# Low halves of weights made by ScalarE and an accumulating DMA instead of VectorE

## The chip, the cores and the metric

The kernel runs on one core of one Trainium2 chip. The metric is the device time of one execution in microseconds (us); a time is the median of several runs. Engines are named as in the profile: PE is TensorE's matrix product, PEld its weight load, DVE VectorE, ACT ScalarE, POOL GpSimd, and SP the engine that issues most of the DMAs.

## The reference

A small diffusion backbone of two layers over 512 latent tokens (and 256 context tokens in layer 0), all in float32. Each layer is FFN, mixer, FFN; the mixer is attention in layer 0 and a gated short convolution in layer 1. Each part has an RMS norm with shift, scale and gate (adaLN) that come from a conditioning vector through a large matrix.

```python
def modulate(x, g, shift, scale):
    return rmsnorm(x, g) * (1 + scale) + shift

def swiglu(x, w_gate, w_up, w_down):
    return (jax.nn.silu(x @ w_gate) * (x @ w_up)) @ w_down

def macaron_ffn(xs, g, shift, scale, gate, w_gate, w_up, w_down):
    return xs + 0.5 * gate * swiglu(modulate(xs, g, shift, scale), w_gate, w_up, w_down)
...
    for i in range(DEPTH):                       # DEPTH = 2
        m = jnp.split((jax.nn.silu(c) @ mod_w[i] + mod_b[i])[:, None, :], N_MOD, axis=-1)
        ...
        x_lat = macaron_ffn(x_lat, norm_g[i, 0], m[0], m[1], m[2], ...)
        ...                                      # attention or convolution, with m[3], m[4], m[5]
        x_lat = macaron_ffn(x_lat, norm_g[i, 2], m[6], m[7], m[8], ...)
    return rmsnorm(x_lat, final_g)
```

The model width is 1024 (8 chunks of 128), the FFN's inner width 2816 (22 chunks of 128).

## The kernel before

Activations lie feature-major: a tile holds 128 features by up to 512 tokens. Every matrix product has float32 precision and is made of three products in the faster float32r type: weight and input are each split into a high part (rounded to float32r) and a low part (the remainder), and PE adds up high x high, high x low and low x high (`mm3`). So each weight tile of 128 x 1024 costs 24 products of 128x128 with 512 tokens.

A weight comes in by `load_w`: SP issues the load into a tile `raw`; ACT writes the high half `wh` (L114); an engine, nearly always DVE, writes the low half `wl` as raw minus high (L115). Each of `raw`, `wh` and `wl` has three buffers. A `raw` buffer is free again when both halves are written, a `wh` or `wl` buffer when PE has done its last product with it.

The FFNs are numbered: 0 and 1 in layer 0, 2 and 3 in layer 1. FFN 1, 2 and 3 work alike, on the latent tokens alone. The 22 inner chunks are cut into blocks of 4, 4, 4, 6 and 4. For each chunk of a block `gate_up` loads a gate and an up weight (two tiles of 1024 columns), lets PE make both products into one PSUM tile `S` (of which there are two), and ACT and DVE make SiLU(gate) x up and split it again (`out`, tiles `P` and `h`). After each block but the last `down` loads the block's part of the down matrix, in 4 units of 1024 columns for a block of 4, in 8 units of 768 columns for the block of 6, and DVE adds the result to `x` (L470). The first three weights of an FFN (`head`), the up weight of chunk 1 (`after_head`) and the last block's down weights (`tail`) go through other functions.

Beside the FFN bodies runs the adaLN work: each `gate_up` of FFN 1 and 2 calls `background(2)`, two steps of `mod_step`. A step loads two tiles of 256 KB of the adaLN matrix (`aux`, four buffers, L197, issued by SP) and DVE sums their products with the conditioning vector (L210). FFN 3 has none.

The code is written in program order; a scheduler places each instruction on its engine's queue by its own estimate of when it can run, so the order of a queue isn't that of the code. Each engine runs its queue strictly in order, and SP issues its DMAs in order too: a load that waits for its buffer holds back all that stand behind it.

Of the kernel before, what the change touches and what calls it, by code (L numbers as in the profile page):

```python
# [18 lines left out]
KD = D // P            # chunks of the model width  # L19
N = 512                # latent tokens  # L20
NC = 256               # context tokens
# [7 lines left out]
BLOCKS = [(0, 4), (4, 4), (8, 4), (12, 6), (18, 4)]   # (first f chunk, chunks)  # L29
BLOCKS0 = [(0, 6), (6, 6), (12, 6), (18, 4)]                  # layer 0, first FFN  # L30
# [11 lines left out]
def build(tc, A, out):  # L42
    """A: name -> DRAM AP (host layouts, see kernel()); out: [128, 8, 512] feature-major."""
# [4 lines left out]
    with ExitStack() as es:  # L48
# [9 lines left out]
        def uid(s):  # L58
# [4 lines left out]
        BUFS = {"xn": 16, "h": 12, "P": 4,                                                 # 3 KB per partition  # L63
                "x": 12, "sc": 2, "pj": 6, "pv": 4, "P1": 4, "aux": 4,                     # 2 KB
                "nh": 7}                                                                   # 1 KB
# [7 lines left out]
        def tmp(n):  # L73
            """temporary of a norm"""
            if n > 256:
                return dt_("pj")
            return dp.tile([P, 256], F32, tag="nh", bufs=BUFS["nh"], name=uid("nh"))

# [16 lines left out]
        wl_eng = [nc.vector]  # L95

        def load_wx(src, tiles, lo):
            """in halves of 512 columns; tiles: two for each part"""
# [10 lines left out]
        def load_w(src, n=1024, eng=None):  # L109
            raw = wp.tile([P, 1024], F32, tag="raw", bufs=3, name=uid("raw"))  # L110
            nc.sync.dma_start(raw[:, :n], src)
            hi = wp.tile([P, 1024], F32R, tag="wh", bufs=3, name=uid("wh"))
            lo = wp.tile([P, 1024], F32R, tag="wl", bufs=3, name=uid("wl"))
            nc.scalar.activation(hi[:, :n], raw[:, :n], AF.Copy)  # L114
            (eng or wl_eng[0]).tensor_tensor(lo[:, :n], raw[:, :n], hi[:, :n], op=ALU.subtract)  # L115
            return hi, lo

        def split(hi, lo, src, scale=None):
            """hi + lo == src * scale exactly (scale a power of two)"""
# [9 lines left out]
        def after_mm(i):  # L129
            """not scheduled before the last matrix product emitted so far"""  # L130
# [4 lines left out]
        def mm3(outs, w, x, segs, first, last):  # L135
            """outs[i] += w^T x[:, segs[i]] with the three products that float32 needs"""
# [17 lines left out]
        wx = [dt_("x", dtype=F32R) for _ in range(4)]           # for weights of the start  # L154
# [4 lines left out]
        def load_c(nm):  # L159
            """silu of the vector on every partition"""  # L160
# [31 lines left out]
        def mod_step(l, m, ch, dve, pool=(), paced=True, early=False):  # L192
            """the streams in dve are summed on the vector engine, those in pool on GpSimd and ScalarE"""
# [38 lines left out]
        def mod_scale(l, m, i, s="c", out=None, ks=slice(0, KD)):  # L232
            """norm_g * (1 + scale)"""
# [6 lines left out]
        def rsqrt(ps, n, width):  # L240
            """(ps / width + eps) ** -0.5, with one Newton step after the table"""
# [10 lines left out]
        class Norm:  # L252
            """sum of squares gathered chunk by chunk (two partial sums), then 1/rms on every partition"""
# [5 lines left out]
            def add(self, xk, pre=False):  # L259
                """pre: have the table of rsqrt loaded by the time the sum is there"""  # L260
                n, i = self.n, min(self.k // 4, 1)
                if self.k >= self.parts:            # summed on the tensor engine
                    i = len(self.ss)
                    self.ss.append(None)
# [17 lines left out]
        def modulate_chunk(k, xk, y, s, b, hi, lo):  # L282
# [3 lines left out]
            if n <= 256 and k % 3 == 2:             # a part of them on ScalarE and GpSimd  # L286
# [12 lines left out]
        class Entry:  # L299
            """the input of a sub-layer: modulated norm of x, one token segment at a time"""  # L300
# [26 lines left out]
        class Head:  # L327
            """first products of a sub-layer, k outermost and one token segment at a time,
            so that they run while the rest of the input is still being made"""

            def __init__(self, units):
                # units: [(weight source, {segment: PSUM})], the PSUM allocated when used
                self.w = [load_w(u[0]) for u in units]
                self.units = units

            def run(self, e, si, ks=range(KD), inner=False):
                """inner: k innermost, so that the weights are freed one after the other"""
# [9 lines left out]
        def transition(e, down, head):  # L347
            """down(si): last products of the sub-layer before, segment si (calls e.norms[si].add);
            head(): makes the Head; statistics and products of neighbouring segments overlap"""
# [26 lines left out]
        def last_proj(e, srcs, nk, hl, evict):  # L376
            """output projection with nk chunks of input: the last three weight units are kept and used
            one token segment at a time"""
# [27 lines left out]
        class FFN:  # L406
# [6 lines left out]
            def head(self):  # L413
                """gate and up of chunk 0, gate of chunk 1"""
# [18 lines left out]
            def gate_up(self, e, f, segs, halves=False):  # L433
                fi = self.fi
                ws = (load_w(A["wg"][fi, f]), load_w(A["wu"][fi, f]))
# [21 lines left out]
            def after_head(self, e):  # L457
                """finish chunk 1 (its up product); returns with chunks 0 and 1 done for the latents"""
# [18 lines left out]
            def down(self, bi):  # L477
# [3 lines left out]
                for d0 in range(0, KD, dpu):  # L481
                    w = load_w(*self.down_src(bi, d0))
# [7 lines left out]
            def body(self, e, first=2):  # L490
                """everything up to the last block's gate and up"""
# [10 lines left out]
            def tail(self, e2):  # L502
                """down products of the last block, one segment at a time"""
# [4 lines left out]
                held = {}                       # the three units loaded last  # L508
# [36 lines left out]
        # ================= layer 0: FFN 0 =================  # L545
        # the latents' part of the first chunks starts as soon as its modulation is there
# [83 lines left out]
        # ================= layer 0: attention =================  # L630
# [13 lines left out]
        # the residual waits in DRAM  # L644
# [4 lines left out]
        # differential lambda on every partition  # L649
# [22 lines left out]
        def proj_fm(src, outs):  # L672
            """outs: (segment, what takes the result) one after the other"""
# [9 lines left out]
        def proj_v(src, res, stack):  # L683
            """256 columns of a value projection, token-major, 3 tiles of 128 tokens per buffer: hi and lo in
            buffers of their own, or (stack) for each head of width 64 side by side, the second head lo first"""
# [30 lines left out]
        # Two heads (or maps) of width 64 share a chunk. For each, the moving operand stacks the  # L716
        # hi and lo parts of k over the 128 rows of the array and the stationary one holds hi of q
        # twice, so that one product gives qh kh + qh kl; ql kh is a second one on 64 rows.
# [3 lines left out]
        def q_parts(q, src, dst, scale):  # L722
            """src: 128 rows; dst: column view to write"""
# [32 lines left out]
        def scores(key, parts):  # L756
            """for (out, m, qs, ks) in parts: out = q k^T of head or map m, query columns qs, key columns given by
            the view ks; the products on 64 rows come together (outs in different banks)"""
# [64 lines left out]
        class Diff:  # L823
            """two query tiles of one differential head"""
# [77 lines left out]
        # neighbourhood heads: token order t' = column * 8 + row; query tiles are  # L902
        # A = columns 0-7 and 56-63, 1 = 8-23, 2 = 24-39, 3 = 40-55, so that tiles 1..3
        # see exactly the key columns 16(j-1) .. 16(j-1)+31 and A sees 0-15 and 48-63.
        def na_bias(h):
            """[128, 512]: columns 0-255 for tiles 1..3, 256-511 for tile A"""
            b = dt_("aux")
            nc.gpsimd.memset(b, -1e30)
            wn = A["rpb"][h]                        # [8 rq, 31 * 8]
# [7 lines left out]
        class Na:  # L917
            """one neighbourhood head: rows 64 i .. of pair pr"""
# [42 lines left out]
            def values(self):  # L961
# [14 lines left out]
                def transposes(step):  # L976
                    pt = acc("pv")
                    dsts = []
                    if step < 2:                        # context keys, all queries
                        src = [Ps[t][:, 256 + step * P:256 + (step + 1) * P] for t in range(4)]  # L980
                        dsts = [(4 + step, 0, N, o)]
                    else:                               # band keys, the two tiles that see the chunk
# [31 lines left out]
                # rows R hold the product with hi of v, the other half that with lo  # L1014
# [10 lines left out]
        def alternate(a, b):  # L1025
            """scores and values in turn, spread evenly: (unit, generator) each"""
# [24 lines left out]
        pos = [0.0, 0.0]                        # time on the tensor engine: attention, projections  # L1051
# [51 lines left out]
        # ================= layer 0: FFN 1 =================  # L1103
# [5 lines left out]
        # ================= layer 1: FFN 0 =================  # L1109
# [7 lines left out]
        # ================= layer 1: short convolution =================  # L1117
# [43 lines left out]
        # ================= layer 1: FFN 1, final norm =================  # L1161
# [100 lines left out]
```

## Time and profile before

| | |
|---|---|
| median of 3 runs | 2298.47 us (2294.9 to 2307.2) |
| span of the profiled execution | 2304.0 us (no other time of that execution is on the page) |
| PE busy | 2224.3 us, 97% of the span |
| DVE, ACT, POOL busy | 60%, 38%, 12% |
| DMA: bytes, mean rate | 279.07 MB, 121 GB/s |
| bodies of FFN 1, 2, 3 in the span, about | 1030 to 1370, 1390 to 1740, 1940 to 2280 us |

A row of a group names line, engine, operation and tiles, then count, busy time and mean of one in ns, then the idle time of the engine just before such instructions and what ended most of it. A row of waits names who waited for what: total us, times, longest. A row of the timeline gives start and duration in us, and in brackets the idle time before it with its releaser.

### The profile page before, as it was taken

What the parts mean: (1) busy time and instruction counts of PE and PEld (TensorE: products, weight loads), DVE (VectorE), ACT (ScalarE), POOL (GpSimd) and SP (SyncE); (2) the same over time, 40 slices, a digit from 0 to 9 for tenths busy, and PEclk for the clock granted to TensorE, in tenths of its full rate; (3) what the DMA queues carried; (4) which work ended last, traced back from release to release, by engine and by line L of the source; (5) the groups of instructions that cost most, each with busy time, mean ns of one, the idle gap of its engine ahead of it and who ended that gap; (6) DMA issues with size and microseconds to landing.
All of it is one profiled execution on the core that took longest, in us unless ns stands there. A gap on an engine that the chain in (4) does not pass through costs nothing.

```text
span 2304.0 us, 30465 instructions
## 1 busy us (share of the span) xinstructions
PE 2224.3 (97%) x11728; PEld 1889.3 (82%) x11728; DVE 1372.8 (60%) x2388; ACT 869.8 (38%) x1489; POOL 284.1 (12%) x196
## 2 busy tenths in 40 slices
PE   5899999999989999999999999999999999999998
PEld 3688888888878788788888888888889889888887
DVE  8893763534788876775555467555437446434335
ACT  4651421212456766652222244222225224222224
POOL 4550520000232311120000010000001001000001
PEclk9999999999999999999999999999999999999999
DMA  7672443434520111315555454444332322333232
GB/s 243 220 230 90 140 133 105 149 103 128 160 69 29 48 39 53 101 48 165 172 169 165 143 163 156 156 159 152 109 107 95 100 93 92 93 100 96 87 109 74
DMA packets 109993, 279.07 MB, mean 121 GB/s; under 512 B 14100, under 2 KB 18452, under 8 KB 109848
## 3 DMA queue, kind: packets, MB, share of 16 engines
q1 hardware_dynamic: 109848, 277.13, 38.5%
q8 instruction: 91, 1.49, 0.3%
q14 instruction: 54, 0.44, 0.1%
HBM read 272.88 MB, written 4.19 MB: 120 GB/s over the span
## 4 chain that ended last, share of the span: by engine, by line
PE 84%; DVE 10%; ACT 3%; issue 2%; POOL 1%; DMA 1%; SPq 0%; DVEq 0%; ACTq 0%; POOLq 0%
PE S L140 39%; PE acc L140 38%; PE acc L694 3%; DVE junk L210 1%; DVE wl L115 1%; PE S L763 1%; DVE xn L292 1%; PE acc L973 1%; DVE sm L215 1%; PE S L761 1%; PE acc L997 1%; DVE nh L285 1%; ACT wh L114 0%; POOL P L205 0%; PE acc L888 0%
## 5 line engine op out<-in xcount | busy, mean ns | idle before, releaser
L140 PE MATMUL S<-xn,wh 128*128 128x512 f32 (+1 forms) x3008 | 924.8, 380 | 20.8 <-ACT xn L291 12.5
L114 ACT ACTIVATE wh<-raw 128x1024 fp32r<-128x1024 f32 (+1 forms) x354 | 364.5, 1031 | 1072.2 <-PE acc L140 516.5
L140 PEld LDWEIGHTS S<-xn,wh 128*128 128x128 f32 x3008 | 555.9, 189 | 135.6 <-ACT xn L291 15.5
L115 DVE TENSOR_TENSOR wl<-raw,wh 128x1024 fp32r<-128x1024 f32 (+1 forms) x331 | 398.8, 1206 | 430.9 <-ACT wh L114 428.1
L140 PE MATMUL S<-xn,wl 128*128 128x512 f32 (+1 forms) x1504 | 569.0, 378 | 6.3 <-DVE wl L115 6.3
L140 PE MATMUL acc<-h,wh 128*128 128x512 f32 (+1 forms) x2148 | 534.6, 347 | 2.9 <-DVE x L470 2.8
L140 PE MATMUL acc<-xn,wh 128*128 128x256 f32 (+1 forms) x1664 | 451.1, 332 | 3.7 <-ACT xn L291 1.6
L140 PEld LDWEIGHTS acc<-h,wh 128*128 128x128 f32 x2148 | 364.2, 190 | 59.4 <-ACT h L121 3.1
L140 PE MATMUL acc<-h,wl 128*128 128x512 f32 (+1 forms) x1074 | 345.0, 344 | 1.4 <-DVE wl L115 1.4
L140 PEld LDWEIGHTS S<-xn,wl 128*128 128x128 f32 x1504 | 285.0, 190 | 61.5 <-DVE wl L115 8.3
L140 PEld LDWEIGHTS acc<-xn,wh 128*128 128x128 f32 x1664 | 297.1, 193 | 32.1 <-issue 2.7
L140 PE MATMUL acc<-xn,wl 128*128 128x256 f32 (+1 forms) x832 | 273.1, 329 | 3.2 <-DVE wl L115 3.2
L470 DVE SCALAR_TENSOR_TENSOR x<-acc,sm,x 128x512 f32<-128x512 f32 (+1 forms) x216 | 132.2, 629 | 220.1 <-PE acc L140 219.8
L140 PEld LDWEIGHTS acc<-h,wl 128*128 128x128 f32 x1074 | 192.4, 189 | 26.4 <-DVE wl L115 1.8
L270 POOL TENSOR_TENSOR nh<-nh,nh 128x256 f32<-128x256 f32 x42 | 45.4, 1085 | 1233.2 <-ACT nh L266 898.8
L210 DVE SCALAR_TENSOR_TENSOR junk<-aux,sc 128x512 bf16<-128x512 f32 x256 | 192.6, 752 | 1.6
L140 PEld LDWEIGHTS acc<-xn,wl 128*128 128x128 f32 x832 | 159.3, 192 | 16.9 <-DVE wl L115 4.1
L205 POOL TENSOR_TENSOR P<-aux,pv 128x512 f32<-128x512 f32 x64 | 106.3, 1674 | 131.5 <-ACT P L208 67.5
L121 ACT ACTIVATE h<-P 128x512 fp32r<-128x512 f32 (+2 forms) x99 | 62.5, 631 | 109.9 <-DVE P L429 109.8
L122 DVE TENSOR_TENSOR h<-P,h 128x512 fp32r<-128x512 f32 (+2 forms) x99 | 76.2, 769 | 20.1 <-ACT h L121 20.1
L694 PE MATMUL acc<-wh,xn 128*128 128x256 f32 x384 | 79.4, 295 | 1.5 <-DVE h L122 1.5
L115 POOL TENSOR_TENSOR wl<-raw,wh 128x1024 fp32r<-128x1024 f32 x23 | 56.7, 2468 | 185.6 <-ACT wh L114 185.6
(177 smaller groups left out, 1760.1 us busy)
## 6 DMA issues: line engine op xcount, KB each, us to landing
aux<-modw SPq DMA_DIRECT2D x288, 256.0 KB
raw<-wu SPq DMA_DIRECT2D x92, 512.0 KB
raw<-wg SPq DMA_DIRECT2D x91, 512.0 KB
raw<-wd SPq DMA_DIRECT2D x59, 512.0 KB
raw<-wd SPq DMA_DIRECT2D x48, 384.0 KB
raw<-cin SPq DMA_DIRECT2D x24, 512.0 KB
h<-modw SPq DMA_DIRECT2D x32, 256.0 KB
raw<-win SPq DMA_DIRECT2D x16, 512.0 KB
```

Of the source, the lines that this page charges most:

```text
L114: nc.scalar.activation(hi[:, :n], raw[:, :n], AF.Copy)
L115: (eng or wl_eng[0]).tensor_tensor(lo[:, :n], raw[:, :n], hi[:, :n], op=ALU.subtract)
L121: nc.scalar.activation(hi, src, AF.Copy)
L122: nc.vector.tensor_tensor(lo, src, hi, op=ALU.subtract)
L140: last_mm[0] = nc.tensor.matmul(o, a, b[:, s0:s1], start=first and ti == 0, stop=last and ti == 2)
L205: nc.gpsimd.tensor_mul(pr, raw, sc[s][h])
L210: i = nc.vector.scalar_tensor_tensor(junk, raw, 1.0, sc[s][h], op0=ALU.mult, op1=ALU.mult, accum_out=a)
L215: nc.vector.scalar_tensor_tensor(o[:, ch:ch + 1], pt[:, 0:1], pt[:, 1:2], modb[:, c:c + 1], op0=ALU.add, op1=ALU.add)
L270: (nc.gpsimd, nc.vector)[i].tensor_add(self.ss[i][:, :n], self.ss[i][:, :n], sq[:, :n])
L285: nc.vector.scalar_tensor_tensor(t[:, :n], xk, s[:, k:k + 1], y, op0=ALU.mult, op1=ALU.mult)
L470: nc.vector.scalar_tensor_tensor(v, ps, g[:, d:d + 1], v, op0=ALU.mult, op1=ALU.add)
L694: last_mm[0] = nc.tensor.matmul(o, a, b, start=k == 0 and ti == 0, stop=k == KD - 1 and ti == 2)
```

## The change

In FFN 1, 2 and 3 the weights that `gate_up` and `down` load take another way to their low half. ACT writes minus raw, rounded to float32r (so minus the high half), into `wl`; a DMA issued by POOL then adds the float32 tile `raw` onto `wl`, so that raw minus high is left; ACT writes the high half as before. FFN 0, the heads, `after_head`, the tails, the attention's and the convolution's weights stay as they are. The comments of the file are gone, and lines move by up to 6.

```diff
-        def load_w(src, n=1024, eng=None):
+        def load_w(src, n=1024, eng=None, add=False):
             raw = wp.tile([P, 1024], F32, tag="raw", bufs=3, name=uid("raw"))
             nc.sync.dma_start(raw[:, :n], src)
             hi = wp.tile([P, 1024], F32R, tag="wh", bufs=3, name=uid("wh"))
             lo = wp.tile([P, 1024], F32R, tag="wl", bufs=3, name=uid("wl"))
+            if add:
+                nc.scalar.activation(lo[:, :n], raw[:, :n], AF.Copy, scale=-1.0)
+                nc.gpsimd.dma_start(lo[:, :n], raw[:, :n], accum_op=ALU.add)
+                nc.scalar.activation(hi[:, :n], raw[:, :n], AF.Copy)
+                return hi, lo
             nc.scalar.activation(hi[:, :n], raw[:, :n], AF.Copy)
...
             def gate_up(self, e, f, segs, halves=False):
                 fi = self.fi
-                ws = (load_w(A["wg"][fi, f]), load_w(A["wu"][fi, f]))
+                ws = (load_w(A["wg"][fi, f], add=fi > 0), load_w(A["wu"][fi, f], add=fi > 0))
...
             def down(self, bi):
...
                 for d0 in range(0, KD, dpu):
-                    w = load_w(*self.down_src(bi, d0))
+                    w = load_w(*self.down_src(bi, d0), add=self.fi > 0)
```

That is 40 gate and up weights and 20 down units in each of the three FFNs: 180 in all, 156 of 1024 columns and 24 of 768. In the orders of the whole program DVE has 180 instructions fewer (1894 for 2074), ACT 180 more (1489 for 1309), POOL 180 DMAs more; SP has the same number.

ACT's queue in the second block of FFN 1, before (`raw1896` and `raw1912` are gate weights, `raw1899` and `raw1915` up weights, `S` the products of an earlier chunk, `P` and `h` its SiLU and split):

```order
L114 ACTIVATE wh1897_10688<-raw1896_10686 128x1024
L428 ACTIVATE P1872_10580<-S1869_10529 128x512
L121 ACTIVATE h1870_10578<-P1872_10580 128x512
L114 ACTIVATE wh1900_10694<-raw1899_10692 128x1024
L114 ACTIVATE wh1913_10772<-raw1912_10770 128x1024
L428 ACTIVATE P1888_10664<-S1885_10613 128x512
L121 ACTIVATE h1886_10662<-P1888_10664 128x512
L114 ACTIVATE wh1916_10778<-raw1915_10776 128x1024
```

The same place after the change:

```order
L118 ACTIVATE wh1897_10700<-raw1896_10698 128x1024
L434 ACTIVATE P1872_10590<-S1869_10539 128x512
L116 ACTIVATE wl1898_10701<-raw1896_10698 128x1024
L127 ACTIVATE h1870_10588<-P1872_10590 128x512
L118 ACTIVATE wh1900_10707<-raw1899_10705 128x1024
L116 ACTIVATE wl1901_10708<-raw1899_10705 128x1024
L118 ACTIVATE wh1913_10786<-raw1912_10784 128x1024
L434 ACTIVATE P1888_10676<-S1885_10625 128x512
L116 ACTIVATE wl1914_10787<-raw1912_10784 128x1024
L127 ACTIVATE h1886_10674<-P1888_10676 128x512
L118 ACTIVATE wh1916_10793<-raw1915_10791 128x1024
L116 ACTIVATE wl1917_10794<-raw1915_10791 128x1024
```

Each weight now has two writes on ACT; the scheduler puts the high half first, and for a gate weight the SiLU of an earlier chunk stands between them.

SP's queue at the same place, before (`aux` are the adaLN loads, `wd` a down unit):

```order
L111 DMA raw1912_10770<-wg 128x1024
L197 DMA aux1889_10669<-modw 128x512
L197 DMA aux1890_10671<-modw 128x512
L111 DMA raw1915_10776<-wu 128x1024
L197 DMA aux1893_10678<-modw 128x512
L197 DMA aux1894_10680<-modw 128x512
L111 DMA raw1928_10854<-wd 128x1024
```

And after:

```order
L112 DMA raw1912_10784<-wg 128x1024
L203 DMA aux1889_10681<-modw 128x512
L203 DMA aux1890_10683<-modw 128x512
L203 DMA aux1893_10690<-modw 128x512
L203 DMA aux1894_10692<-modw 128x512
L112 DMA raw1915_10791<-wu 128x1024
L112 DMA raw1928_10870<-wd 128x1024
```

The load of the up weight has moved behind the second pair of adaLN loads.

## The prediction

> **What bounds the kernel now.** I read the page's first part, then the stretches of the later FFNs, then the waits in them, and only then the engines that feed TensorE there. In the rows of stretches the columns are: the stretch, its length, busy time and count of PE, PEld, DVE, ACT, POOL, then the granted clock, the mean share of the 16 DMA engines in use, and GB/s.
>
> ```profile
> span 2304.0 us, 30465 instructions
> PE 2224.3 (97%) x11728; PEld 1889.3 (82%) x11728; DVE 1372.8 (60%) x2388; ACT 869.8 (38%) x1489; POOL 284.1 (12%) x196
> ...
> 1040.00:1360.00 320.00, 320.00 (x1420) 264.40 (x1419) 180.50 (x342) 85.68 (x102) 0.00 (x0) 1.00 0.53 165
> 1400.00:1640.00 240.00, 240.00 (x1063) 197.94 (x1063) 137.98 (x256) 67.73 (x80) 0.00 (x0) 1.00 0.50 159
> 1640.00:1740.00 100.00, 99.93 (x500) 84.86 (x499) 40.34 (x56) 31.01 (x45) 2.83 (x3) 1.00 0.32 97
> 1960.00:2280.00 320.00, 319.98 (x1453) 265.54 (x1452) 124.16 (x142) 90.64 (x117) 2.85 (x3) 1.00 0.31 94
> ```
>
> The four stretches are the bodies of the three FFNs that the change touches (layer 0 FFN 1, layer 1 FFN 0 in two parts, layer 1 FFN 1). PE is busy for 320.00 of 320.00 us, 240.00 of 240.00, 99.93 of 100.00 and 319.98 of 320.00, at a granted clock of 1.00. DVE, which the change relieves, is busy for 57% there and less. What PE still waits for after 1200 us:
>
> ```profile
> PE S L140 <- DVE wl L115: 0.5, 2, 0.3
> PE S L140 <- POOL xn L289: 0.5, 2, 0.3
> PE acc L140 <- DVE wl L115: 0.3, 1, 0.3
> PE acc L140 <- ACT wh L114: 0.3, 1, 0.3
> PE acc L140 <- DVE x L470: 0.2, 1, 0.2
> ```
>
> All waits of PE for DVE's low halves come to 0.8 us in 1100 us. So there is nothing to win in the place that is changed; the question is only whether the new way of making a low half still arrives in time, and whether the DMA engines can carry it.
>
> **What is removed and added.** By the order of instructions, 180 low halves move: 156 of 1024 columns and 24 of 768.
>
> ```profile
> L114 ACT ACTIVATE wh<-raw 128x1024 fp32r<-128x1024 f32 (+1 forms) x354 | 364.5, 1031 | 1072.2 <-PE acc L140 516.5
> L115 DVE TENSOR_TENSOR wl<-raw,wh 128x1024 fp32r<-128x1024 f32 (+1 forms) x331 | 398.8, 1206 | 430.9 <-ACT wh L114 428.1
> ```
>
> DVE loses 180 x 1.206 = 217 us, which is worth 0 to 0.8 us of the end (the waits above). ACT gains 180 writes that I price like its conversion of the same tile, 180 x 1.031 = 186 us. Over 1100 us of touched stretches that adds 17% to an ACT that is busy for 27% (85.68 of 320); it has room, and its price shows only in the latency below. POOL gets 180 DMA issues; in these stretches it is busy for 0 to 3% and nothing that PE needs is queued behind them in a body (the norm's additions and the last chunks of the modulated input stand before or after the whole run of DMAs in POOL's order).
>
> **The latency of a low half.** A weight's slots come free when PE is done with the weight three before it, so a pair must be finished within two weights' time.
>
> ```profile
> 1301.79 0.85 ACT L114 ACTIVATE wh<-raw 128x768 fp32r<-128x768 f32 x1 [3.23 <-PE acc L140]
> 1305.87 1.06 ACT L114 ACTIVATE wh<-raw 128x1024 fp32r<-128x1024 f32 x1 [3.23 <-PE acc L140]
> 1309.95 1.06 ACT L114 ACTIVATE wh<-raw 128x1024 fp32r<-128x1024 f32 x1 [3.02 <-PE acc L140]
> 1319.47 1.06 ACT L114 ACTIVATE wh<-raw 128x1024 fp32r<-128x1024 f32 x1 [4.38 <-PE S L140]
> 1324.91 1.06 ACT L114 ACTIVATE wh<-raw 128x1024 fp32r<-128x1024 f32 x1 [4.38 <-PE S L140]
> 1325.88 0.58 ACT L428 ACTIVATE P<-S 128x512 f32<-128x512 f32 x1
> ...
> 1306.96 1.23 DVE L115 TENSOR_TENSOR wl<-raw,wh 128x1024 fp32r<-128x1024 f32 x1
> 1314.06 0.61 PE L140 MATMUL S<-xn,wh 128*128 128x512 f32 x2
> ```
>
> PE takes 1324.91 - 1319.47 = 5.44 us for a weight of 1024 columns and 4.08 us (1305.87 - 1301.79) for one of 768. The gate weight converted at 1305.87 is first used at 1314.06, 8.19 us later; its low half was there at 1308.19, with 5.87 us to spare. After the change ACT writes hi (1.06), then sometimes a SiLU (0.58), then minus hi (1.06): the order shows hi first, although the code has it last. What is left for the issue on POOL and the accumulating DMA is 10.88 - 2.12 - 0.58 = 8.18 us among gate and up weights, 8.16 - 1.70 = 6.46 us among the short units, and 8.19 - 2.12 = 6.07 us for the first gate behind them.
>
> The trace of before has no accumulating DMA and none issued by POOL. The nearest row is a load of the same 512 KB that ACT had to wait for:
>
> ```profile
> 126.37 0.33 SPq L111 DMA_DIRECT2D raw<-wg  x1
> 127.51 0.33 SPq L111 DMA_DIRECT2D raw<-wu  x1
> 131.44 1.06 ACT L114 ACTIVATE wh<-raw 128x1024 fp32r<-128x1024 f32 x1 [1.48 <-DMA raw<-wg]
> ```
>
> That is 5.07 us from issue to use with a second load beside it. It is the low end: an accumulate does no less than a load. It would fit everywhere (6.07 at the tightest). An accumulate must read raw and also read what stands in the low tile, through the same engines. In the first FFN stretch 165 GB/s go with a share of 0.53, so 311 GB/s fill the engines, and 512 KB (524,288 bytes) take 1.69 us of all 16. With a second reading I get 5.07 + 1.69 = 6.76 us: inside 8.18, 0.69 us over at the first gate behind the short units, once in each FFN. That is 2 us. For the short units 5.07 + 1.27 = 6.34 is inside 6.46. The high end is a third pass (two reads and a write one after the other), 8.45 us, which is over in every place.
>
> **The load on the DMA engines.** This is the larger term. In each FFN the added weights are 52 of 1024 columns and 8 of 768, 30.4 MB, and PE takes 52 x 5.44 + 8 x 4.08 = 315.5 us for them: one pass of the accumulates is 96 GB/s, as long as PE is not held up. The stretches carry that much in weight loads already (94 GB/s at 1960 us, where there is nothing else); the first two also carry the adaLN weights:
>
> ```profile
> L197 SPq DMA_DIRECT2D aux<-modw x84: 327/328/878, 1040.9 to 1362.3; - x84
> L197 SPq DMA_DIRECT2D aux<-modw x56: 327/328/1019, 1406.4 to 1619.3; - x56
> ...
> 0.00:58.00 58.00, 33.52 (x94) 20.85 (x95) 49.27 (x86) 26.25 (x54) 25.02 (x23) 0.97 0.73 244
> ```
>
> The last row is the busiest stretch of the program: 244 GB/s at a share of 0.73, by which 334 GB/s fill the engines. The FFN rows give less (165/0.53 = 311, 94/0.31 = 303). With 334:
> - One pass: 165 + 96 = 261 GB/s, 78%. No cost.
> - Two passes: 165 + 192 = 357, 107% over 320 us, 22 us; at 1400 us 159 + 192 = 351, 105% over 240 us, 12 us; at 1640 and 1960 us 289 and 286, both under 334, nothing. Sum 34 us.
> - Three passes: 453 (+114 us), 447 (+81), 385 (+15), 382 (+46): 256 us.
>
> I take two, since one would mean that reading the old low tile is free and three would mean that nothing overlaps. The bounds of two passes: with 311 and 318 GB/s from the stretches' own rows it is 15% of 320 and 10% of 240 us, 72 us; below, the two readings are in SBUF, and the share of a load may hold its wait for HBM, so 0. I keep 34, between both.
>
> The Trainium skill, Collectives: The Full Stack, "The bandwidth ceiling: the fold count and why AG ≠ RS ≠ AR", says that an add in the DMA path costs no cycles of its own, but that it needs two source reads on one ring, so that a reduce runs at half the rate of a copy (ratio 1.93). By that page it is two passes, and the 34 us stand; no row here shows it.
>
> **Raw tiles and SP.** A raw tile is now given back when the accumulate is done, not when DVE is done.
>
> ```profile
> SPq L111 <- DVE wl L115: 607.3, 141, 15.8
> 1303.66 0.33 SPq L111 DMA_DIRECT2D raw<-wg  x1
> 1314.03 1.06 ACT L114 ACTIVATE wh<-raw 128x1024 fp32r<-128x1024 f32 x1 [3.02 <-PE acc L140]
> ```
>
> SP already waits for that release. The load issued at 1303.66 is converted at 1314.03, 10.37 us later, of which about 5 are the load; the release moves by some 1.06 + 6.76 - 1.23 = 6.6 us, so with two passes the slack of 5.3 is used up on the tight weights, but three raw tiles give a round of 3 x 5.44 = 16.3 us against 5.07 + 2.12 + 0.58 + 6.76 = 14.5. I cost it at 0; the cover is 1.8 us, and it is gone as soon as the accumulate takes 8.6 us. Behind a raw load that waits, SP now has up to four adaLN loads in a row; DVE's sums over them come later, but their results are wanted only at the next gate or norm, so also 0.
>
> **The sum.** 34 (DMA engines full) + 2 (first gate) - 0.8 (waits for DVE) = 35 us. Against the profiled execution: its span of 2304.0 + 35 = 2339. The page gives no other time of that execution; its span lies 5.5 us above the median of the three runs, 2298.5, and the forecast is for the median: 2298.5 + 35, about 2333 us.
>
> **The rivals.**
> - The accumulate is hidden: not slower. Its place is the same 60 weights of each FFN; it holds as long as an accumulate costs fewer than (334 - 165)/96 = 1.8 passes of the engines and under 6.07 us. For it: the one load that was waited for took 5.07 us, and the engines stand at 0.31 to 0.53. Against it: two operands are read. It gives 2298.5 + 0 to 4, about 2300 us. The Trainium skill, DMA: Bandwidth & Descriptors, "Anatomy of one DMA — SWDGE (gpsimd) path", gives 2.0 us plus bytes over 436 GB/s for a DMA issued from GpSimd, an estimate of 3.2 us here; by that page this rival is the one. Chance 0.29.
> - The accumulate is slow, three passes or more: every low half is late, the round of a raw tile is 5.07 + 2.12 + 0.58 + 8.45 = 16.2 us, as long as PE's three weights, and the DMA engines are over full in all three FFNs. 2298.5 + 256, some 2555 us, with everything between 2375 and that for accumulates between two passes and three. For it: no row excludes it. Chance 0.27.
> - Faster: DVE, less busy, makes the modulated inputs at the seams between sub-layers sooner. The change leaves the low halves at the seams on DVE, and PE's waits for DVE in all of the last 1100 us are 1.0 us. It would have to take over 11.5 us. Chance 0.03.
>
> The forecast itself (two passes, the engines full beside the adaLN loads) has 0.41, and by its bounds reaches from 2310 (what is slower at all by the bound below) to 2298.5 + 72 + 2, some 2375 us. About 0.5%, 11.5 us, is what a measurement of this kernel can tell from no change. Slower by more than that is 0.41 + 0.27 = 0.68, within it 0.29, faster 0.03. The range from 2294 to 2480 us takes in the hidden case, all of the forecast and the nearer part of the slow one; it leaves out about 0.17 above and 0.02 below.
>
> **What would show it.** In the profile after: DVE's group of low halves at 151 instructions instead of 331 and ACT up by 180. PE waits whose releaser is a DMA of POOL's queue (or DVE evictions falling behind), in the FFN stretches at 1040 and 1400 and hardly in the one at 1960; there the DMA share near 1.0. If the share stays under 0.85 and PE at 100%, the accumulate is one pass and the first rival holds. If PE waits in the FFN without adaLN loads as well, it is the slow one. The forecast is also wrong if POOL needs several us to issue each DMA: then PE waits while the DMA engines are not full.

## The result, and the profile after

The changed kernel takes 2335.02 us (median of four runs, 2328.69 to 2344.6) against 2297.49: 1.0152 times as long, 95% interval 1.0125 to 1.0179, or 35 us more by the ratio and 37.5 by the medians. The forecast was 2333, 35 above its base. Most of it comes from the place that was named, but two of its terms were off in opposite directions, as the experiments show.

The page of the kernel after: span, busy time, DMA queues (packets, MB, share of 16 engines over the span), the issue on POOL, and the median us from issue to landing.

```profile
span 2326.7 us, 30941 instructions
PE 2225.0 (96%) x11728; PEld 1884.9 (81%) x11728; DVE 1169.3 (50%) x2208; ACT 1031.1 (44%) x1669; POOL 437.4 (19%) x376
...
q1 hardware_dynamic: 109848, 277.13, 36.8%
q0 software_dynamic: 25920, 91.24, 21.4%
...
L117 POOL DMA_DIRECT2D wl<-raw x180 | 155.4, 864 | 822.0 <-ACT wl L116 782.9
...
wl<-raw POOLq DMA_DIRECT2D x156, 512.0 KB, 6.3
wl<-raw POOLq DMA_DIRECT2D x24, 384.0 KB, 4.7
```

DVE lost 204 us of work (217 were reckoned) and ACT gained 161 (186); as sums of work neither shows in the time. POOL issues each accumulate in 0.864 us; in the median one of 1024 columns lands 6.3 us after its issue (6.76 was the estimate, from issue to use). The 91.24 MB are the 180 low tiles counted once, although an addition has two operands to read.

The same stretches as before, with the same columns; PE busy is the first number after the length, the last two are the DMA share and GB/s:

```profile
1040.00:1360.00 320.00, 313.91 (x1375) 255.02 (x1374) 108.68 (x263) 134.06 (x156) 49.10 (x57) 1.00 0.96 248
1400.00:1640.00 240.00, 228.25 (x995) 184.72 (x994) 81.17 (x196) 102.21 (x116) 36.28 (x42) 0.99 0.92 236
1640.00:1740.00 100.00, 99.10 (x436) 81.26 (x435) 19.71 (x33) 41.31 (x50) 15.52 (x18) 1.00 0.85 202
1960.00:2280.00 320.00, 317.90 (x1423) 262.24 (x1422) 54.34 (x76) 140.43 (x164) 52.09 (x61) 1.00 0.83 188
```

Where adaLN loads run, the DMA engines are at 0.96 and 0.92 (0.53 and 0.50 before), and PE, never idle there before, now is for 6.1 and 11.8 us. In the last FFN, without such loads, the share is 0.83 and PE loses 2.1 us. The idle time is less than the loss: FFN 1 takes 13.0 us longer in this trace (table below), and PE is idle for 6.1 us of its stretch. One wait, 2.2 us, lies ahead of the stretch, and the records of two products overlap (each lasts 0.39 us, the next starts 0.23 us after it), so a stop of PE shows only in part. PE's largest waits after 1000 us, and DVE's largest between 1030 and 1750 us:

```profile
PE S L146 <- DMA wl<-raw: 11.6, 14, 3.0
PE acc L146 <- ACT h L127: 5.0, 4, 2.0
PE acc L146 <- DMA wl<-raw: 3.8, 4, 2.4
PE S L146 <- POOL xn L295: 2.9, 4, 1.7
PE acc L146 <- DVE h L128: 2.7, 3, 1.7
...
DVE junk L216 <- DMA aux<-modw: 181.5, 57, 8.2
```

Low halves that have not landed: 15.4 us. Splits `h` that come late: 7.7 us. (The wait for `xn` is no new one: 2.2 us before.) DVE now stands for 181.5 us in front of adaLN loads that are still on their way; before, it had no such wait. How that reaches PE is seen in FFN 2, where the product `P` stands behind the sums in DVE's queue:

```profile
1434.60 0.69 DVE L216 SCALAR_TENSOR_TENSOR junk<-aux,sc 128x512 bf16<-128x512 f32 x1 [7.41 <-DMA aux<-modw]
...
1436.82 0.68 DVE L435 TENSOR_TENSOR P<-P,S 128x512 f32<-128x512 f32 x1
...
1437.54 0.63 ACT L127 ACTIVATE h<-P 128x512 fp32r<-128x512 f32 x1 [1.04 <-DVE P L435]
...
1438.22 0.96 PE L146 MATMUL acc<-h,wh 128*128 128x512 f32 x3 [1.43 <-ACT h L127]
```

All five waits for splits in FFN 2, 6.8 of the 7.7 us, stand behind such a row; the low halves cost PE 5.7 us there.

To compare places I take the time between the same two products of the three FFNs in each trace (products counted in order of time: 5480 to 7220, 7350 to 8900, 10000 to 11600). The ratio is to the kernel before, timed beside each run:

| kernel | FFN 1 | FFN 2 | FFN 3 | ratio of times, interval |
|---|---|---|---|---|
| before (two profiles) | 368.8, 368.5 | 338.2, 339.7 | 344.6, 344.5 | |
| after (two profiles) | 381.8, 387.4 | 356.3, 355.1 | 347.1, 348.3 | 1.0152, 1.0125 to 1.0179 |
| narrow adaLN loads | 373.0 | 343.6 | 347.7 | 1.0057, 1.0035 to 1.0079 |
| FFN 3 alone | 368.5 | 339.7 | 348.0 | 1.0023, 1.0008 to 1.0037 |
| FFN 3 alone, two gates left out | 368.6 | 338.1 | 344.9 | 1.0006, 0.9991 to 1.0021 |
| narrow loads and two gates left out | 369.9 | 338.6 | 345.2 | 0.9996, 0.9981 to 1.0011 |
| two gates left out | 385.3 | 349.9 | 344.3 | 1.0107, 1.0059 to 1.0154 |
| plain copy | 369.8 | 339.8 | 344.4 | 1.0019, 0.9999 to 1.0039 |
| up weights alone | 368.8 | 339.7 | 344.6 | 0.9997, 0.9979 to 1.0016 |
| accumulates as pure load | 383.2 | 344.3 | 344.7 | 1.0134, 1.0109 to 1.0160 |
| four raw tiles | 384.4 | 353.8 | 347.9 | 1.0162, 1.0136 to 1.0188 |
| sums a chunk later | 385.5 | 349.3 | 348.4 | 1.0141, 1.0115 to 1.0167 |

The first spans differ by only 22.7 us because FFN 0, which the change doesn't touch, ran 10 us faster in the profile after; the second pair of profiles has 2304.6 and 2342.8 us.

### The profile page after: what moved, and what is told of

The parts are those of the page before. It is cut to its first block, busy times and chain, and to the rows that moved or that the text cites. A ratio compares the mean times of both kernels' runs of the same rounds, so it can differ in the third digit from the quotient of the medians.

```text
span 2326.7 us, 30941 instructions
## 1 busy us (share of the span) xinstructions
PE 2225.0 (96%) x11728; PEld 1884.9 (81%) x11728; DVE 1169.3 (50%) x2208; ACT 1031.1 (44%) x1669; POOL 437.4 (19%) x376
## 3 DMA queue, kind: packets, MB, share of 16 engines
q0 software_dynamic: 25920, 91.24, 21.4%
## 4 chain that ended last, share of the span: by engine, by line
PE 68%; DMA 11%; DVE 10%; issue 5%; ACT 3%; POOL 1%; SPq 0%; DVEq 0%; POOLq 0%; ACTq 0%
PE acc L146 34%; PE S L146 28%; DMA wl<-raw 7%; PE acc L700 3%; DMA raw<-wu 2%; DMA aux<-modw 2%; DVE junk L216 2%; DVE wl L121 1%; PE S L769 1%; DMA raw<-wd 1%; PE acc L979 1%; DVE xn L298 1%; PE acc L1003 1%; PE S L767 1%; DVE sm L221 1%
## 5 line engine op out<-in xcount | busy, mean ns | idle before, releaser
L146 PE MATMUL acc<-h,wl 128*128 128x512 f32 (+1 forms) x1074 | 344.9, 345 | 5.3 <-DMA wl<-raw 3.8
L117 POOL DMA_DIRECT2D wl<-raw x180 | 155.4, 864 | 822.0 <-ACT wl L116 782.9
L216 DVE SCALAR_TENSOR_TENSOR junk<-aux,sc 128x512 bf16<-128x512 f32 x256 | 192.2, 751 | 182.7 <-DMA aux<-modw 181.5
L121 DVE TENSOR_TENSOR wl<-raw,wh 128x1024 fp32r<-128x1024 f32 (+1 forms) x151 | 185.0, 1228 | 108.5 <-ACT wh L120 107.7
L435 DVE TENSOR_TENSOR P<-P,S 128x512 f32<-128x512 f32 (+1 forms) x91 | 60.3, 662 | 308.0 <-ACT P L434 307.2
L116 ACT ACTIVATE wl<-raw 128x1024 fp32r<-128x1024 f32 (+1 forms) x180 | 183.2, 1018 | 16.4 <-DMA raw<-wu 16.4
```

The lines of the kernel that those rows point to most:

```text
L116: nc.scalar.activation(lo[:, :n], raw[:, :n], AF.Copy, scale=-1.0)
L117: nc.gpsimd.dma_start(lo[:, :n], raw[:, :n], accum_op=ALU.add)
L146: last_mm[0] = nc.tensor.matmul(o, a, b[:, s0:s1], start=first and ti == 0, stop=last and ti == 2)
L216: i = nc.vector.scalar_tensor_tensor(junk, raw, 1.0, sc[s][h], op0=ALU.mult, op1=ALU.mult, accum_out=a)
L435: nc.vector.tensor_mul(sl[:, s0:s1], sl[:, s0:s1], uu)
```

## The experiments

**Narrow adaLN loads: nearly no bytes.**

```diff
+        wid = [N]
...
-                nc.sync.dma_start(raw, A["modw"][l, m, :, ch, h * N:(h + 1) * N])
+                nc.sync.dma_start(raw[:, :wid[0]], A["modw"][l, m, :, ch, h * N:h * N + wid[0]])
...
-                        i = nc.vector.scalar_tensor_tensor(junk, raw, 1.0, sc[s][h],
+                        i = nc.vector.scalar_tensor_tensor(junk[:, :wid[0]], raw[:, :wid[0]], 1.0, sc[s][h][:, :wid[0]],
...
+        wid[0] = 16
         f1 = FFN(1, False, gates_fn(0, 8, False), 2)
```

> The changed kernel, but each adaLN load issued in FFN 1 and 2 brings 16 columns instead of 512 (and DVE sums over 16): the loads keep their number and their place in SP's queue, their bytes are gone; the adaLN vectors of layer 1 are therefore only partial sums. Theory A (the DMA engines are full beside the adaLN loads): the slowdown goes, within 6 us of the kernel before, DMA share in FFN 1 under 0.85. Theory B (a low half comes too late by its own latency, whatever else is on the DMA engines): still 25 to 38 us slower. Theory C (the up weight's load stands behind four adaLN loads in SP's queue, which wait for DVE): still 15 to 38 us slower.

The slowdown fell from 1.0152 to 1.0057: about 22 of 35 us went, and 13 stayed (8 to 18 by the interval), more than theory A allowed. B, with its 25 us or more, is out as the main cause; C's least, 15 us, lies within the interval, so this run alone doesn't rule it out. Two runs below do, as a cause by itself: the plain copy and the narrow loads with two gates left out keep SP's order of four adaLN loads before the up weight, and lose 0.2% and nothing. The edit also shortens DVE's sums (DVE is busy for 76.02 us of FFN 1's stretch, not 108.68), so the 22 us are the bytes and these sums together; the plain copy keeps the sums whole. In the stretch of FFN 1, and then all of PE's waits for low halves in `S`, by time:

```profile
1040.00:1360.00 320.00, 316.67 (x1391) 260.10 (x1391) 76.02 (x277) 135.55 (x158) 49.81 (x59) 1.00 0.88 195
...
PE S L146 <- DMA wl<-raw: 8.6, 5, 2.5
...
1042.90 0.50 PE L146 MATMUL S<-xn,wl 128*128 128x512 f32 x1 [2.02 <-DMA wl<-raw]
1317.55 0.50 PE L146 MATMUL S<-xn,wl 128*128 128x512 f32 x1 [1.31 <-DMA wl<-raw]
1414.83 0.50 PE L146 MATMUL S<-xn,wl 128*128 128x512 f32 x1 [2.54 <-DMA wl<-raw]
1963.31 0.50 PE L146 MATMUL S<-xn,wl 128*128 128x512 f32 x1 [1.40 <-DMA wl<-raw]
2237.95 0.50 PE L146 MATMUL S<-xn,wl 128*128 128x512 f32 x1 [1.34 <-DMA wl<-raw]
```

The share is 0.88 (theory A said under 0.85), PE waits for low halves at these five places and once for 0.5 us at a down unit, and by the table each FFN still loses some 3 to 5 us. DVE still stands for 137.0 us in front of adaLN loads, and PE waits for no split: its standing costs PE only where it outlasts the time that a split has to spare.

**The change in FFN 3 alone.**

```diff
-                ws = (load_w(A["wg"][fi, f], add=fi > 0), load_w(A["wu"][fi, f], add=fi > 0))
+                ws = (load_w(A["wg"][fi, f], add=fi > 2), load_w(A["wu"][fi, f], add=fi > 2))
```

(and the same in `down`).

> The change in FFN 3 alone, where there are no adaLN loads: 60 accumulates instead of 180. Theory A: 0 to 4 us slower than the kernel before, DMA share in FFN 3 about 0.83 as in the changed kernel. Theory B: a third of the slowdown, about 12 us. Theory C: nothing, as no adaLN load stands there.

It is 1.0023 times as long, 5 us (2 to 9 by the interval; 3.5 us in FFN 3 by the table), about A's bound and under B's 12. The waits say where; first the beginning of FFN 3's body (start, duration):

```profile
1948.33 1.06 ACT L118 ACTIVATE wh<-raw 128x1024 fp32r<-128x1024 f32 x1 [0.38 <-PE S L146]
1949.41 1.28 ACT L434 ACT_TABLE_LOAD   x1
1950.70 0.60 ACT L434 ACTIVATE P<-S 128x512 f32<-128x512 f32 x1
1951.20 1.05 ACT L116 ACTIVATE wl<-raw 128x1024 fp32r<-128x1024 f32 x1
...
1952.57 1.01 POOL L117 DMA_DIRECT2D wl<-raw  x1 [8.51 <-ACT wl L116]
...
1957.30 0.50 PE L146 MATMUL S<-xn,wl 128*128 128x512 f32 x1 [1.52 <-DMA wl<-raw]
```

This is the gate weight of chunk 2, the first that is added. Between its high half and its minus-high half ACT loads a table and makes a SiLU, so that the accumulate is issued 4.2 us after the conversion began, and PE stands. The second place is the gate of chunk 18, the first behind the short down units:

```profile
2222.81 1.04 ACT L116 ACTIVATE wl<-raw 128x1024 fp32r<-128x1024 f32 x1
...
2224.15 0.86 POOL L117 DMA_DIRECT2D wl<-raw  x1 [3.65 <-ACT wl L116]
...
2231.78 0.50 PE L146 MATMUL S<-xn,wl 128*128 128x512 f32 x1 [1.18 <-DMA wl<-raw]
```

Here the accumulate takes 7.6 us from issue to use. These are the only two waits for a low half in this run.

**FFN 3 alone, without these two gates.** The edit is shown against the kernel of FFN 3 alone.

```diff
-                ws = (load_w(A["wg"][fi, f], add=fi > 2), load_w(A["wu"][fi, f], add=fi > 2))
+                ws = (load_w(A["wg"][fi, f], add=fi > 2 and f not in (2, 18)), load_w(A["wu"][fi, f], add=fi > 2))
```

> The change in FFN 3 alone, and there without the gate weights of chunks 2 and 18 (the first of the body, and the first behind the short down units): 58 accumulates. The FFN 3 alone kernel took 348.0 us for 1600 products of FFN 3 where the kernel before takes 344.5. If the remaining cost is the latency of those two low halves alone: 344.5 to 345.2, PE's waits for wl gone. If it is spread over all weights: 347 to 348.

FFN 3 takes 344.9 us instead of 348.0, and the time is 1.0006 of the kernel before, which is no measurable difference. All that FFN 3 lost hung on two of its 60 low halves.

**Both together, and the gates alone in the whole change.**

```diff
-                ws = (load_w(A["wg"][fi, f], add=fi > 0), load_w(A["wu"][fi, f], add=fi > 0))
+                ws = (load_w(A["wg"][fi, f], add=fi > 0 and f not in (2, 18)), load_w(A["wu"][fi, f], add=fi > 0))
```

once with the narrow adaLN loads:

> The changed kernel with the narrow adaLN loads (16 columns in FFN 1 and 2, so the adaLN vectors of layer 1 are partial sums) and without the gate weights of chunks 2 and 18 of each FFN: 174 accumulates. If the cost is the sum of the adaLN loads' bytes and these two latencies and nothing else: within 5 us of the kernel before. If something else is left: 8 to 13 us slower, as with the narrow loads alone.

and once with the full ones:

> The changed kernel without the gate weights of chunks 2 and 18 of each FFN, adaLN loads as they are: 174 accumulates. If the two costs add: 10 to 13 us of the 37 go, 22 to 28 us slower. If a full DMA makes others late in their place: 32 to 38 us slower.

With both gone the 174 accumulates that are left cost nothing that can be measured (0.9996; FFN 1 and FFN 3 within 1.4 and 0.7 us, FFN 2 as before, and PE waits 0.5 us for a low half in all). Between the narrow loads with these gates and without them lie 14 us by the ratios and 10.6 by the table. With the adaLN loads back it is 1.0107, 25 us by the ratio, but the interval reaches from 14 to 36, so that the two costs add is likely and not sharply shown; the first time is the firm one. In that last kernel FFN 3 is back at 344.3 us, and PE's largest waits are:

```profile
PE S L146 <- DMA wl<-raw: 6.8, 10, 1.6
PE acc L146 <- ACT h L127: 5.6, 6, 2.0
PE acc L146 <- DVE h L128: 4.6, 4, 1.7
```

With the gates gone, the late splits (10.2 us) stop PE for longer than the late low halves (6.8, and 1.3 more at down units).

**A copy instead of the addition: one reading less.**

```diff
-                nc.gpsimd.dma_start(lo[:, :n], raw[:, :n], accum_op=ALU.add)
+                nc.gpsimd.dma_start(lo[:, :n], raw[:, :n])
```

> The changed kernel, but the DMA that POOL issues copies raw into the low tile instead of adding to it: the same number of DMAs, the same waits, one reading less; the low half is then the whole weight. Theory A: one pass of the engines instead of nearly two; DMA share in FFN 1 falls from 0.96 to some 0.8, landing from 6.3 us to 4 to 5, and the time is within 8 us of the kernel before. Theory B: the landing is shorter by 1 to 2 us, so part of the slowdown goes, 10 to 25 us stay. Theory C: nothing changes, 30 to 38 us slower.

The slowdown is gone but for 0.2%, and the interval touches none:

```profile
1040.00:1360.00 320.00, 319.98 (x1450) 266.11 (x1449) 116.49 (x280) 138.83 (x166) 33.16 (x60) 1.00 0.79 256
...
q0 software_dynamic: 25920, 91.24, 11.1%
...
wl<-raw POOLq DMA_DIRECT2D x156, 512.0 KB, 3.8
```

The same packets and bytes take 11.1% of a span of 2301.0 us instead of 21.4% of 2326.7, so adding costs 497.9/255.4 = 1.95 times the engines' time of copying. It also lands 2.5 us sooner, and PE's waits for low halves fall to 1.4 us, the two gates included; so this run prices the second reading but doesn't separate load from latency. The narrow loads do that, but for the shorter sums.

**The accumulates as pure load.** The edit is against the kernel before; `gate_up` and `down` pass `add` as in the change.

```diff
             (eng or wl_eng[0]).tensor_tensor(lo[:, :n], raw[:, :n], hi[:, :n], op=ALU.subtract)
+            if add:
+                for i in range(2):
+                    nc.gpsimd.dma_start(acd[i][:, :n // 2], lo[:, i * n // 2:(i + 1) * n // 2], accum_op=ALU.add)
```

> The kernel before (DVE makes every low half), and beside it the same 180 accumulates as pure load: for each of these weights POOL issues two accumulates of half its columns from the finished low tile onto a scratch tile that nobody reads. raw tiles come free as before. For the space the P tiles are 3 instead of 4, the norm's small ones 6 instead of 7. Theory A: the DMA engines fill up all the same, raw and adaLN loads come late: 15 to 40 us slower than the kernel before. Theories B and C: nobody waits for these DMAs, within 4 us of the kernel before.

It is 1.0134 times as long although DVE makes every low half as before and nothing is computed from the accumulates. FFN 1 loses 14.6 us, FFN 2 some 5, FFN 3 none. That is 20 of the 31 us; between FFN 0 and FFN 1 (products 3000 to 5480), where there are no accumulates, this kernel and the one with four raw tiles take 421.1 us each and the others 412.8 to 417.8, so the smaller buffers that these two share probably cost some 6 us.

```profile
1040.00:1360.00 320.00, 314.08 (x1374) 258.15 (x1373) 171.79 (x323) 84.01 (x101) 98.89 (x115) 0.99 1.00 248
...
PE acc L147 <- ACT h L128: 15.1, 8, 4.9
...
DVE wl L119 <- DMA acd<-wl: 131.4, 56, 4.5
```

The engines are at 1.00. The kernel is not as pure as meant: beside adaLN loads DVE waits 131.4 us until an accumulate has read the tile that it wants to write, and PE's largest wait is for `h`, not for a low half. FFN 3 has the same accumulates, no such wait of DVE and no loss. So the run shows that the accumulates cost time only beside the adaLN loads, but not how much of it is that wait, which the changed kernel doesn't have.

**Up weights alone: a third of the accumulates.**

```diff
-                ws = (load_w(A["wg"][fi, f], add=fi > 0), load_w(A["wu"][fi, f], add=fi > 0))
+                ws = (load_w(A["wg"][fi, f]), load_w(A["wu"][fi, f], add=fi > 0))
```

(and no addition in `down`).

> The change for the up weights alone: 60 accumulates, 20 in each FFN, all of 1024 columns. Theory A: the engines have room (share in FFN 1 about 0.7), 0 to 4 us slower than the kernel before. Theory B: a third of the accumulates, about 12 us slower.

0.9997, and 0.65 for the DMA share of FFN 1 (0.45 in FFN 3's stretch). With room on the engines the accumulate lands in 4.6 us, and it costs nothing that can be measured:

```profile
1040.00:1360.00 320.00, 320.00 (x1454) 265.72 (x1453) 158.82 (x323) 105.96 (x129) 19.42 (x22) 1.00 0.65 196
...
wl<-raw POOLq DMA_DIRECT2D x60, 512.0 KB, 4.6
```

**Four raw tiles.**

```diff
-            raw = wp.tile([P, 1024], F32, tag="raw", bufs=3, name=uid("raw"))
+            raw = wp.tile([P, 1024], F32, tag="raw", bufs=4, name=uid("raw"))
```

> The changed kernel with four raw tiles instead of three (for the space the P tiles are 3 instead of 4, the norm's small ones 6 instead of 7). Theory A (the DMA engines are full): no buffer makes room on them, still 25 to 40 us slower than the kernel before. Theory D (the round of a raw tile is too long because it is given back only after the accumulate): the raw loads start earlier, 0 to 12 us slower.

1.0162, of which some 6 us probably belong to the smaller buffers (see the pure load); the three FFNs take 1086.1 us together, with three tiles 1085.2 and 1090.8. A fourth tile gives nothing back: the round of a raw tile was not what was missing.

**Sums a chunk later.** DVE's sums over the adaLN loads are kept back until the next call.

```diff
+        def flush():
+            while pend:
+                pend.pop(0)()
...
+            if late[0]:
+                pend.append(sums)
+            else:
+                sums()
...
         def background(n):
+            flush()
             for _ in range(n):
```

> The changed kernel, but from FFN 1 on DVE's sums over a pair of adaLN loads come one gate_up call after the call that issued the loads, with the same bytes and the same accumulates, so that DVE doesn't stand in front of a load that is still on its way. Theory A alone (bytes: low halves and raw tiles land late): PE's waits for wl stay at some 15 us, 30 to 38 us slower than the kernel before. Theory E (a part of the slowdown is DVE, which waits 181.5 us for adaLN loads and holds back the SiLU products and splits queued behind): PE's waits for ACT and DVE h L127, L128 (7.7 us) go, 22 to 30 us slower.

1.0141, and DVE's wait stayed: the scheduler moved the loads later together with the sums (from the issue of a load to its sum 6.9 us in the median, 7.1 without the edit).

```profile
DVE junk L223 <- DMA aux<-modw: 178.0, 55, 8.0
```

So the run doesn't tell how much DVE's standing costs; that stays open.

**Both kernels once more, for FFN 0.**

> The kernel before once more, for its profile: in the two profiles at hand FFN 0, whose code the change doesn't touch, takes 441.9 us for 2500 products before and 433.3 us after. If that is a property of the execution, this profile shows some other value; if it belongs to the program, it shows 441.9 again.

> The changed kernel once more, for its profile: FFN 0 as above (433.3 again if it belongs to the program), and the DMA share in FFN 1 and 2 at 0.9 to 1.0 again.

Between products 500 and 3000 the first two profiles have 440.9 us before and 430.8 after (not quite the figures that the expectations name), the new ones 441.0 for the kernel before and 441.4 for the changed one. The changed kernel has shown both, so it belongs to the execution, not to the program. The DMA share of the changed kernel is 0.95 and 0.87 in its second profile.

## Why the prediction came out, by its steps

- **Nothing to win.** Right: less work on DVE made no kernel faster, and the 60 additions for up weights, all hidden, left the time as it was.
- **Two passes of the engines.** Right, now measured: 1.95. The sentence cited from the Trainium skill, Collectives: The Full Stack, "The bandwidth ceiling: the fold count and why AG ≠ RS ≠ AR" (an add reads two sources and runs at half a copy's rate, 1.93, measured there on a collective) agrees with this case's 1.95.
- **Engines full beside the adaLN loads, 34 us.** The place and the cause are right: the shares are 0.96 and 0.92 there, and the time goes with the loads' bytes. The size was too high: 1.0152 falls to 1.0057, about 22 us, and 25 with the gates left out. The way to PE was only half foreseen: late low halves, but also late splits through DVE (below).
- **The first gate behind the short units, 2 us in all.** About right as far as it went: with narrow loads PE waits 1.3 us at this gate (chunk 18) in FFN 1 and in FFN 3 and not at all in FFN 2, though the accumulate took 7.6 us from issue to use in the run of FFN 3 alone, not 6.76. What the sum lacked is the gate of chunk 2, which was not looked at: at the beginning of a body a table load and a SiLU stand on ACT between the two writes of its tile, and PE waits 2.0, 2.5 and 1.4 us there. Both gates together are worth 11 to 14 us (by the table, by the ratios); how that divides is known only from the waits.
- These errors, 34 instead of about 22 and 2 instead of 11 to 14, nearly cancel. That the total of 35 fits so well is luck: its two large parts were off.
- **Raw tiles, 0.** Borne out: a fourth tile gave nothing back.
- **Later adaLN sums on DVE, 0.** This step failed. I asked when their results are wanted, and not what stands behind them in DVE's queue: 181.5 us of waiting, with the SiLU products and splits behind it, and 6.8 us of PE's waits in FFN 2 follow from it by the rows shown. It is a part of what the full engines cost, not a cost beside it: with narrow loads these waits are gone. How much would be left without it is open.
- **The rivals.** The hidden one fails with all 180 but holds with 60 additions, where the engines have room. The three-pass one is out by 1.95; its sign, PE waiting in the FFN without adaLN loads, was worded too widely, as PE does wait there, 2.1 us at two gates. The estimate of 3.2 us cited from the Trainium skill, DMA: Bandwidth & Descriptors, "Anatomy of one DMA — SWDGE (gpsimd) path", compares with 3.8 us for the plain copy here; for the addition, 4.6 to 6.3 us, it doesn't hold.

## What to carry to other kernels

When an engine is taken out of work that it did off the critical path, ask what the replacement loads: an addition in a DMA uses the DMA engines nearly twice as long as a copy, and its bytes are counted once, so read the share of the engines and not the GB/s. Check the first and the last weight of each run of buffers by themselves: here 58 of 60 low halves of FFN 3 had time to spare, and two gates made the whole cost where the engines had room. And for a load that comes later, look at what waits behind its reader, not only at who wants the result.

## What the runs showed of the hardware

- An accumulating DMA of 128x1024 float32 within SBUF took 0.86 us to issue on POOL; in the median it landed in 4.6 us at DMA shares of 0.43 to 0.65 and in 6.3 at 0.83 to 0.96. A copy of the same size took 0.53 us and 3.8, at 0.53 to 0.81.
- FFN 0 ran at different speeds in executions of the same program: the changed kernel took 430.8 us for 2500 products in one profile and 441.4 in the other, with a granted clock of 1.00 between 193 and 547 us and PE busy all that time in both. Over all kernels six profiles lie at 430.8 to 432.2 us, seven at 440.0 to 442.6 and one at 434.9. What sets it was not found; two single profiles can differ by some 10 us through it.
